# Second mixer of a three-layer fp32 kernel: q's norm moves into the softmax's exponential, the projections run q0, k, q1, v, the output weights' splits stand behind q's rotation, and the sine products read PSUM

## The chip, the cores and the metric

One core of one Trainium2 chip runs one program. The metric is the time of one execution in device microseconds; lower is better. Measurements of this kernel are told apart here from about 0.2% on (2.0 us).

## The reference, cut to what matters

The program is a chain of three layers on 256 tokens of 1024 channels, all in fp32. The change lies in the second layer's mixer, a grouped-query attention with 16 query heads and 4 key/value heads of 64 channels:

```python
def odd_mixer(x, mix_norm, w_qkv, q_norm, k_norm, w_out):
    Bsz, S, _ = x.shape
    proj = rms_norm(x, mix_norm) @ w_qkv
    q, k, v = jnp.split(proj, [GQA_Q_WIDTH, GQA_Q_WIDTH + GQA_KV_WIDTH], axis=-1)
    q = rms_norm(q.reshape(Bsz, S, GQA_HEADS, GQA_HEAD_DIM), q_norm)
    k = rms_norm(k.reshape(Bsz, S, GQA_KV_HEADS, GQA_HEAD_DIM), k_norm)
    v = v.reshape(Bsz, S, GQA_KV_HEADS, GQA_HEAD_DIM)
    cos, sin = axial_rope_tables(S)
    q = apply_rope(q, cos, sin)
    k = apply_rope(k, cos, sin)
    return gqa_block_attention(q, k, v) @ w_out
```

`rms_norm` divides each head by the root of its mean square (one factor per token and head) and multiplies by a gain; `apply_rope` turns neighbouring channels by an angle: a cosine product of each channel plus a sine product of its neighbour. The attention is softmax(q kT / 8) v over all 256 keys. After the mixer comes the layer's feed-forward block.

## The kernel before, in words

The tokens are two tiles of 128 (t = 0, 1). Every fp32 product with weights is made of three PE matmuls in fp32r (`mm3`, L121 to L123): weights and activations are each split into a rounded half (`wh`, `xTh`) and the rest (`wl`, `xTl`). `wload` (L103) loads four 128-row blocks of weights per DMA on SP's queue (`raw`, 3 buffers), then splits them in pairs: a cast on ACT (L112) and a subtraction on DVE (L113), into 6 buffers. `gemm` (L153) walks the 8 blocks of the 1024 input channels; at the end of each it calls `tick`, which runs work put off by `defer`, and at its end `done(t, acc)`.

The second mixer (L797 to L923) projects in three passes of 512 columns: k and v together (`okv`), then heads 0 to 7 of q (`oq`, c = 0), then heads 8 to 15 (c = 1). Each pass's `done` copies the sum out of PSUM with the token's norm as a factor (L840, L866), and `rope` (L813) squares it on ACT, sums the squares on DVE (L820), takes the power -1/2 on POOL (`gp_rms`, L188), makes the cosine products on POOL (L826) and the two halves of the sine products on DVE (L828), both from that copy in SBUF. The put-off `mid` adds the two (L870) and multiplies by the norm (L871; for k L848, twice). The put-off `fin` transposes on PE (`tq` L877, `tk` L854) and splits the result into `qS` (ACT cast L881, DVE subtraction L882) or `kh`, `kl`.

A unit of attention (`ga_unit` L888, `attn_unit` L309) handles two heads of one token tile: scores on PE (`sc_ga` L895, 2 PSUM buffers), negated maximum on DVE (`mx_ga` L328), exponential on ACT with the maximum as bias and a row sum (`p_ga` L335), reciprocal on DVE (L337), four transposes on PE (`pt_ga` L343), a copy on ACT (`pT_ga` L345), the value matmuls on PE (`o_ga` L354) and the scaled output on DVE (`ot` L356). `tq`, `tk`, `pt_ga` and `o_ga` share 2 PSUM buffers. `pipeline` runs 16 units, the three phases of a unit 0, 1 and 2 slots apart. After every four units `split_T` transposes their output (`tp_ot`, `mo`). The output projection (`oo`, weights `w_out_o`) fills in between units from the 13th slot on and ends the stage. The first two units start when 6 of the 8 blocks of the last projection are done.

The framework's scheduler fixes each engine's order when the kernel is built; every engine then works its queue off in order and waits at its head.

## Time and profile before

| | |
|---|---|
| median of 3 runs (lowest to highest) | 1008.73 us (1006.83 to 1009.10) |
| the profiled execution, its own time | 1009.89 us |
| span of that execution | 1008.1 us |
| PE busy | 978.6 us, 97% of the span |
| DVE, ACT, POOL busy | 65%, 56%, 10% |
| mean granted TensorE clock | 0.988 of full speed |
| second mixer, first projection matmul to the next layer's first | 399.95 to 503.70 us |

A span is the time from the first to the last instruction; the execution's own time is 1.8 us longer. A share of busy time is an average over stages with different limits, so what the change touches is read in the mixer's own stretch. The granted clock is 1.0 at the full 2.4 GHz and 0.5 at 1.2 GHz; a PE that is busy at half clock moves at half speed.

### The profile page before, as it was taken

What the parts mean: (1) busy time and instruction counts of PE and PEld (TensorE: products, weight loads), DVE (VectorE), ACT (ScalarE), POOL (GpSimd) and SP (SyncE); (2) the same over time, 40 slices, a digit from 0 to 9 for tenths busy, and PEclk for the clock granted to TensorE, in tenths of its full rate; (3) what the DMA queues carried; (4) which work ended last, traced back from release to release, by engine and by line L of the source; (5) the groups of instructions that cost most, each with busy time, mean ns of one, the idle gap of its engine ahead of it and who ended that gap; (6) DMA issues with size and microseconds to landing.
All of it is one profiled execution on the core that took longest, in us unless ns stands there. A gap on an engine that the chain in (4) does not pass through costs nothing.

```text
span 1008.1 us, 13120 instructions
## 1 busy us (share of the span) xinstructions
PE 978.6 (97%) x4926; PEld 816.5 (81%) x4926; DVE 650.9 (65%) x1038; ACT 560.6 (56%) x973; POOL 97.5 (10%) x161
## 2 busy tenths in 40 slices
PE   5999999999999999979999999999999999999998
PEld 4888888788888888869888888888888888888876
DVE  5668789776666555776676666555555976665455
ACT  6565778664445444567565444344675854454442
POOL 3130223110000001440010000001000300000000
PEclk9899999999999999989999999999999999999999
DMA  8546321545555455421345545546633565554541
GB/s 325 181 127 243 130 86 42 208 167 185 190 177 199 151 184 209 167 84 43 126 167 172 203 172 197 183 132 244 223 107 105 187 231 188 179 196 153 188 161 42
DMA packets 30535, 167.68 MB, mean 166 GB/s; under 512 B 3048, under 2 KB 8424, under 8 KB 12552
## 3 DMA queue, kind: packets, MB, share of 16 engines
q1 hardware_dynamic: 30472, 166.84, 47.8%
q8 instruction: 39, 0.64, 0.3%
q14 instruction: 24, 0.20, 0.1%
HBM read 165.71 MB, written 1.11 MB: 165 GB/s over the span
## 4 chain that ended last, share of the span: by engine, by line
PE 85%; DVE 7%; POOL 3%; issue 2%; ACT 2%; DMA 1%; SPq 0%; DVEq 0%; POOLq 0%; ACTq 0%
PE acc_fau L123 4%; PE acc_fbu L123 4%; PE acc_fau L122 4%; PE acc_fcu L122 4%; PE acc_fbu L122 4%; PE acc_fcu L121 4%; PE acc_fbu L121 4%; PE acc_fau L121 4%; PE acc_fcu L123 4%; PE acc_mpd L122 2%; PE acc_odd L123 2%; PE acc_mpd L123 2%; PE acc_mpd L121 2%; PE acc_odd L121 2%; PE acc_odd L122 2%; PE acc_fd L122 2%
## 5 line engine op out<-in xcount | busy, mean ns | idle before, releaser
L113 DVE TENSOR_TENSOR wl_fau<-raw_fau,wh_fau 128x1024 fp32r<-128x1024 f32 x44 | 53.8, 1223 | 39.8 <-ACT wh_fau L112 39.8
L113 DVE TENSOR_TENSOR wl_fbu<-raw_fbu,wh_fbu 128x1024 fp32r<-128x1024 f32 x44 | 53.8, 1223 | 39.0 <-ACT wh_fbu L112 39.0
L113 DVE TENSOR_TENSOR wl_fcu<-raw_fcu,wh_fcu 128x1024 fp32r<-128x1024 f32 x44 | 53.6, 1221 | 30.2 <-ACT wh_fcu L112 30.1
L123 PE MATMUL acc_fau<-wh_fau,xTl_f 128*128 128x512 f32 x176 | 70.6, 401 | 0.0
L123 PE MATMUL acc_fbu<-wh_fbu,xTl_f 128*128 128x512 f32 x176 | 70.5, 401 | 0.0
L123 PE MATMUL acc_fcu<-wh_fcu,xTl_f 128*128 128x512 f32 x176 | 70.0, 399 | 0.0
L112 ACT CAST wh_fau<-raw_fau 128x1024 fp32r<-128x1024 f32 x44 | 46.2, 1049 | 41.3 <-PE acc_fau L123 33.1
L122 PE MATMUL acc_fau<-wl_fau,xTh_f 128*128 128x512 f32 x176 | 68.9, 391 | 0.0
L122 PE MATMUL acc_fbu<-wl_fbu,xTh_f 128*128 128x512 f32 x176 | 68.8, 391 | 0.0
L121 PE MATMUL acc_fcu<-wh_fcu,xTh_f 128*128 128x512 f32 x176 | 68.8, 391 | 0.0
L122 PE MATMUL acc_fcu<-wl_fcu,xTh_f 128*128 128x512 f32 x176 | 68.7, 392 | 0.0
L121 PE MATMUL acc_fbu<-wh_fbu,xTh_f 128*128 128x512 f32 x176 | 68.7, 390 | 0.0
L121 PE MATMUL acc_fau<-wh_fau,xTh_f 128*128 128x512 f32 x176 | 68.7, 390 | 0.0
L112 ACT CAST wh_fbu<-raw_fbu 128x1024 fp32r<-128x1024 f32 x44 | 46.2, 1050 | 39.4 <-PE acc_fbu L123 32.9
L112 ACT CAST wh_fcu<-raw_fcu 128x1024 fp32r<-128x1024 f32 x44 | 46.3, 1053 | 30.3 <-PE acc_fcu L123 30.1
L113 DVE TENSOR_TENSOR wl_fd<-raw_fd,wh_fd 128x1024 fp32r<-128x1024 f32 x22 | 26.9, 1224 | 27.4 <-ACT wh_fd L112 27.4
L113 DVE TENSOR_TENSOR wl_mpd<-raw_mpd,wh_mpd 128x1024 fp32r<-128x1024 f32 x22 | 26.9, 1224 | 26.4 <-ACT wh_mpd L112 26.4
L113 DVE TENSOR_TENSOR wl_odd<-raw_odd,wh_odd 128x1024 fp32r<-128x1024 f32 x22 | 26.9, 1224 | 26.4 <-ACT wh_odd L112 26.4
L112 ACT CAST wh_fd<-raw_fd 128x1024 fp32r<-128x1024 f32 x22 | 23.1, 1049 | 29.4 <-PE acc_fd L123 24.1
L466 PE MATMUL xbc<-h,wh_xbc 128*128 128x256 f32 x128 | 38.9, 304 | 0.5 <-DVE xp L476 0.3
L112 ACT CAST wh_mpd<-raw_mpd 128x1024 fp32r<-128x1024 f32 x22 | 23.1, 1048 | 29.2 <-PE acc_mpd L123 23.9
L112 ACT CAST wh_odd<-raw_odd 128x1024 fp32r<-128x1024 f32 x22 | 23.1, 1049 | 29.2 <-PE acc_odd L123 23.9
(506 smaller groups left out, 2830.9 us busy)
## 6 DMA issues: line engine op xcount, KB each, us to landing
raw_fau<-in_w_dram SPq DMA_DIRECT2D x22, 1024.0 KB, 5.0
raw_fbu<-in_w_dram SPq DMA_DIRECT2D x22, 1024.0 KB, 5.2
raw_fcu<-in_w_gu_dram SPq DMA_DIRECT2D x22, 1024.0 KB, 5.0
raw_odd<-in_w_dram SPq DMA_DIRECT2D x10, 1024.0 KB, 4.9
raw_mpd<-in_w_dram SPq DMA_DIRECT2D x10, 1024.0 KB, 4.8
raw_fd<-in_w_dn_dram SPq DMA_DIRECT2D x10, 1024.0 KB, 4.9
raw_xbc<-in_w_xbc_dram SPq DMA_DIRECT2D x8, 1024.0 KB, 5.2
raw_eo<-in_w_out_e_dram SPq DMA_DIRECT2D x6, 1024.0 KB, 5.2
```

Source lines behind the costliest of these rows:

```text
L112: act.copy(wh[:, 0:n, 0:cols], raw[:, i:i + n, 0:cols])
L113: vec.tensor_tensor(out=wl[:, 0:n, 0:cols], in0=raw[:, i:i + n, 0:cols], in1=wh[:, 0:n, 0:cols].bitcast(F32), op=ALU.subtract)
L121: pe.matmul(acc, lhsT=x2[0], rhs=w2[0], start=start, stop=False)
L122: pe.matmul(acc, lhsT=x2[0], rhs=w2[1], start=False, stop=False)
L123: pe.matmul(acc, lhsT=x2[1], rhs=w2[0], start=False, stop=stop)
L466: pe.matmul(d, lhsT=wh[:, cs], rhs=h0[:, k, :], start=k == 0, stop=False)
```

## The change

It does six things, all in the second mixer:

- q is no longer multiplied by its norm. The norm (`rq8`) becomes the scale of the exponential (`scl`, `fac`), and the maximum is multiplied by it on POOL (`nb`, one small operation per unit).
- The sine products read the projection's sum in PSUM, not its copy; the tokens' norm is multiplied into the sine tables instead (four operations on POOL). They are written ahead of the square and its sum.
- The projections run in the order q heads 0 to 7 (512 columns), k (256 columns), q heads 8 to 15, v (256 columns); the first two units start after 6 of v's 8 blocks. `vv` becomes a tile of its own. k's second copy is made by ACT.
- The DVE subtractions of the output weights' first four pairs in each half (`ogen(0)`) are queued behind DVE's last subtraction of `qS`, c = 1 (`issue_after`, `last[1]`); their ACT casts are not.
- The put-off steps of q and k come at other ticks.
- The phases of a unit lie 0, 2 and 3 slots apart.

```diff
-    def wload(src, k0, kn, nm, cols=512):
+    def wload(src, k0, kn, nm, cols=512, behind=None):
...
-            vec.tensor_tensor(out=wl[:, 0:n, 0:cols], in0=raw[:, i:i + n, 0:cols],
-                              in1=wh[:, 0:n, 0:cols].bitcast(F32), op=ALU.subtract)
+            with tc.issue_after(behind) if behind is not None else nullcontext():
+                vec.tensor_tensor(out=wl[:, 0:n, 0:cols], in0=raw[:, i:i + n, 0:cols],
+                                  in1=wh[:, 0:n, 0:cols].bitcast(F32), op=ALU.subtract)
...
+            fac = [sign, sign]
+            if scl is not None:
+                nb = sm.tile([P, 2], F32, tag="nb", name=f"nb_{nm}", bufs=4)
+                gp.tensor_tensor(out=nb, in0=mx, in1=scl(), op=ALU.mult)
+                mx, fac = nb, [scl()[:, h:h + 1] for h in range(2)]
             for h in range(2):
-                act.activation(pvw[:, h, :], src[:, h, :], AF.Exp, bias=mx[:, h:h + 1], scale=sign,
+                act.activation(pvw[:, h, :], src[:, h, :], AF.Exp, bias=mx[:, h:h + 1], scale=fac[h],
                                accum_out=su[:, h:h + 1])
...
+                gp.tensor_scalar(out=S[:, t, :], in0=S[:, t, :], scalar1=rr[t], scalar2=None, op0=ALU.mult)
+
+        def rope(acc, src, nh, t, tab, nm):
...
+            for e in range(2):
+                vec.tensor_tensor(out=tv[:, :, e::2], in0=acc[:, :, 1 - e::2],
+                                  in1=S[:, t, e::2].unsqueeze(1).to_broadcast([P, nh, 32]), op=ALU.mult)
+            gp.tensor_tensor(out=qv, in0=src, in1=C[:, t, :].unsqueeze(1).to_broadcast([P, nh, 64]), op=ALU.mult)
...
-                for e in range(2):
-                    vec.tensor_tensor(out=kd[:, :, e, :], in0=qv, in1=r8, op=ALU.mult)
+                vec.tensor_tensor(out=kd[:, :, 0, :], in0=qv, in1=r8.unsqueeze(2).to_broadcast([P, 4, 64]), op=ALU.mult)
+                act.copy(kd[:, :, 1, :], kd[:, :, 0, :])
                 defer(3, fin)
...
-            defer(4, mid)
+            defer(2 + t, mid)
...
                 def mid():
                     vec.tensor_tensor(out=qv, in0=qv, in1=tv, op=ALU.add)
-                    vec.tensor_tensor(out=qv, in0=qv, in1=r8, op=ALU.mult)
-                    defer(2, fin)
+                    defer(1, fin)
...
-                        vec.tensor_tensor(out=qS[c][e][lo, t], in0=tv[hi], in1=qS[c][e][hi, t].bitcast(F32),
-                                          op=ALU.subtract)
-                defer(3 + 2 * t, mid)
+                        last[c] = vec.tensor_tensor(out=qS[c][e][lo, t], in0=tv[hi],
+                                                    in1=qS[c][e][hi, t].bitcast(F32), op=ALU.subtract).ins
+                defer(2 + 2 * t, mid)
...
-        run(gemm(a["w_qkv_o"][0], KD, xf, done_kv, "okv"))
-        run(gemm(a["w_qkv_o"][1], KD, xf, done_q(0), "oq0"))
-        og = gemm(a["w_qkv_o"][2], KD, xf, done_q(1), "oq1")
+                yield from gemm(a["w_out_o"][n], KD, xT_acc(mo), done, f"oo{n}", kfirst=k0, klast=k0 + 4, accs=accs[n],
+                                behind=lambda: last[1] if k0 == 0 else None)
+
+        run(gemm(a["w_q_o"][0], KD, xf, done_q(0), "oq0"))
+        run(gemm(a["w_k_o"][0], KD, xf, done_k, "ok", cols=256))
+        run(gemm(a["w_q_o"][1], KD, xf, done_q(1), "oq1"))
+        og = gemm(a["w_v_o"][0], KD, xf, done_v, "ov", cols=256)
         run(og, 6)
         ga = pipeline([ga_unit(c, t, pr) for c in range(2) for t in range(NT) for pr in range(4 * c, 4 * c + 4)],
-                      (0, 1, 2))
+                      (0, 2, 3))
```

How the change moves instructions, in each engine's fixed order. Outside the second mixer the orders are the same. The lines of the changed kernel lie 2 to 22 further down.

**DVE, q's rotation and what follows it.** Before, heads 0 to 7: the two products with the norm, then three subtractions of output weights (`wl_oo`) ahead of and between those of `qS`, and only then the first maxima.

```order
L871 TENSOR_TENSOR rq_q_0_3970<-rq_q_0_3970,r_q_0_3967 128x512
L871 TENSOR_TENSOR rq_q_1_3985<-rq_q_1_3985,r_q_1_3982 128x512
L113 TENSOR_TENSOR wl_oo_2_4461<-raw_oo_0_4454,wh_oo_2_4460 128x1024
L113 TENSOR_TENSOR wl_oo_0_4586<-raw_oo_0_4583,wh_oo_0_4585 128x1024
L882 TENSOR_TENSOR qS_3752<-tq_0_4030,qS_3752 64x512
L113 TENSOR_TENSOR wl_oo_2_4590<-raw_oo_0_4583,wh_oo_2_4589 128x1024
L882 TENSOR_TENSOR qS_3753<-tq_0_4030,qS_3753 64x512
L328 TENSOR_REDUCE mx_ga_0_4076<-sc_ga_0_4070 128x2
L882 TENSOR_TENSOR qS_3752<-tq_1_4061,qS_3752 64x512
L328 TENSOR_REDUCE mx_ga_1_4088<-sc_ga_1_4082 128x2
L337 RECIPROCAL su_ga_0_4077<-su_ga_0_4077 128x2
```

Changed, heads 8 to 15, with what each row waits for: the sine products (`rt_q`) read `acc_oq` and wait for ACT, whose copy reads the same PSUM tile; the sums (`rq_q`) wait for POOL's cosine products; no product with the norm follows.

```order
L836 TENSOR_TENSOR rt_q_0_4089<-acc_oq_0_3996,Sgq 128x256 [waits Activation_49]
L836 TENSOR_TENSOR rt_q_0_4089<-acc_oq_0_3996,Sgq 128x256
L836 TENSOR_TENSOR rt_q_1_4104<-acc_oq_1_3997,Sgq 128x256 [waits Activation_49]
L843 TENSOR_REDUCE s_q_0_4095<-rj_q_0_4093 128x8 [waits Activation_49]
L836 TENSOR_TENSOR rt_q_1_4104<-acc_oq_1_3997,Sgq 128x256
L890 TENSOR_TENSOR rq_q_0_4088<-rq_q_0_4088,rt_q_0_4089 128x512 [waits DVE_49,Pool_49]
L843 TENSOR_REDUCE s_q_1_4110<-rj_q_1_4108 128x8 [waits Activation_49]
L890 TENSOR_TENSOR rq_q_1_4103<-rq_q_1_4103,rt_q_1_4104 128x512 [waits DVE_49,Pool_49]
```

The rows right behind these, also of the changed kernel: first maxima, q's four subtractions, and from there the output weights' subtractions between the maxima.

```order
L331 TENSOR_REDUCE mx_ga_0_4200<-sc_ga_0_4194 128x2 [waits PE_49]
L901 TENSOR_TENSOR qS_3760<-tq_0_4141,qS_3760 64x512 [waits Activation_49]
L901 TENSOR_TENSOR qS_3760<-tq_1_4163,qS_3760 64x512 [waits Activation_49]
L331 TENSOR_REDUCE mx_ga_1_4214<-sc_ga_1_4208 128x2 [waits PE_49]
L901 TENSOR_TENSOR qS_3761<-tq_0_4141,qS_3761 64x512 [waits Activation_49]
L901 TENSOR_TENSOR qS_3761<-tq_1_4163,qS_3761 64x512 [waits Activation_49]
L345 RECIPROCAL su_ga_0_4201<-su_ga_0_4201 128x2 [waits Activation_49]
L115 TENSOR_TENSOR wl_oo_0_4544<-raw_oo_0_4541,wh_oo_0_4543 128x1024 [waits DMAHW1_49]
L345 RECIPROCAL su_ga_1_4215<-su_ga_1_4215 128x2 [waits Activation_49]
L331 TENSOR_REDUCE mx_ga_2_4242<-sc_ga_2_4236 128x2 [waits PE_49]
L331 TENSOR_REDUCE mx_ga_3_4263<-sc_ga_3_4257 128x2 [waits PE_49]
```

What moved: before, splits of the output weights stood ahead of the first units' q; now they stand in the middle of the first units, six of them between the third and the tenth unit's rows.

**PE, the opening of the attention.** Before, the transposes of q's second tile are followed at once by the first scores, with matmuls of the last projection between the units.

```order
L877 MATMUL tq_1_4061<-cst,rq_q_1_3985 128x128 x4
L895 MATMUL sc_ga_0_4070<-kh,qS_3752 128x256
L895 MATMUL sc_ga_0_4070<-kl,qS_3752 128x256
L895 MATMUL sc_ga_0_4070<-kh,qS_3752 128x256
L895 MATMUL sc_ga_0_4070<-kl,qS_3752 128x256
L121 MATMUL acc_oq_0_3990<-wh_oq_6_4045,xTh_od 128x512
L122 MATMUL acc_oq_0_3990<-wl_oq_6_4046,xTh_od 128x512
L895 MATMUL sc_ga_1_4082<-kh,qS_3753 128x256
```

Changed, the end of v's projection and what follows: the weights' transposes (`pt_ga`) and the third unit's scores, with no projection matmul left to stand between them until the output projection's first rows, some fifty rows further on.

```order
L123 MATMUL acc_ov_4117<-wh_ov_4178,xTh_od 128x256
L124 MATMUL acc_ov_4117<-wl_ov_4179,xTh_od 128x256
L125 MATMUL acc_ov_4117<-wh_ov_4178,xTl_od 128x256
L351 MATMUL pt_ga_0_4250<-cst,p_ga_0_4199 128x128
L914 MATMUL sc_ga_2_4236<-kh,qS_3758 128x256
L914 MATMUL sc_ga_2_4236<-kl,qS_3758 128x256
L914 MATMUL sc_ga_2_4236<-kh,qS_3758 128x256
L914 MATMUL sc_ga_2_4236<-kl,qS_3758 128x256
L351 MATMUL pt_ga_0_4250<-cst,p_ga_0_4199 128x128 x3
L351 MATMUL pt_ga_1_4271<-cst,p_ga_1_4213 128x128 x2
```

ACT in the same place of the changed kernel: between the transposes of heads 8 to 15 and the end of the first unit's second exponential stand four casts of q and one of the output weights.

```order
L900 CAST qS_3760<-tq_0_4141 64x512 [waits PE_49]
L900 CAST qS_3760<-tq_1_4163 64x512 [waits PE_49]
L113 CAST wh_oo_4_4738<-raw_oo_4_4736 128x1024 [waits DMAHW3_49]
L343 ACTIVATE p_ga_0_4199,su_ga_0_4201<-sc_ga_0_4194,nb_ga_0_4203,r_q_0_3855 128x256 [waits Pool_49]
L900 CAST qS_3761<-tq_0_4141 64x512 [waits DVE_49]
L900 CAST qS_3761<-tq_1_4163 64x512 [waits DVE_49]
L343 ACTIVATE p_ga_0_4199,su_ga_0_4201<-sc_ga_0_4194,nb_ga_0_4203,r_q_0_3855 128x256
```

What moved: the first units no longer wait for their own q (it was turned a projection earlier), but the projection matmuls that stood between units are spent before them.

## Rows read from the trace of the kernel before

**Rows 1.** The table of busy time by stretch: first the whole second mixer, from its first projection matmul to the first matmul of the next feed-forward layer. Columns: the stretch (us from the span's start), its length, then busy time and number of instructions of PE, of PE's weight loads, of DVE, ACT and POOL, the granted TensorE clock as a share of full speed, the busy share of the DMA engines, GB/s.

```profile
399.95:503.70 103.75, 98.52 (x554) 84.77 (x553) 73.10 (x133) 65.86 (x149) 25.37 (x35) 0.93 0.31 106
```

**Rows 2.** The same table for four stretches inside it.

```profile
428.80:438.10 9.30, 5.43 (x29) 3.87 (x27) 7.36 (x10) 4.12 (x6) 3.05 (x3) 0.97 0.31 102
438.10:444.20 6.10, 6.10 (x18) 4.97 (x19) 4.07 (x7) 4.12 (x12) 0.20 (x1) 0.50 0.53 191
444.20:451.20 7.00, 5.63 (x44) 5.06 (x43) 6.26 (x14) 5.77 (x15) 5.43 (x6) 0.99 0.00 0
451.20:457.50 6.30, 6.30 (x32) 6.26 (x31) 4.16 (x10) 2.89 (x10) 1.10 (x1) 0.50 0.00 0
```

**Rows 3.** The list of what PE waited for between 398 and 506 us (engine, line, what it waited for: us in total, times, longest), whole.

```profile
PE sc_ga L895 <- DVE qS L882: 2.4, 2, 1.6
PE tq L877 <- DVE rq_q L871: 1.5, 1, 1.5
PE o_ga L354 <- DVE ot L356: 0.9, 1, 0.9
PE pt_ga L343 <- DVE ot L356: 0.5, 1, 0.5
```

**Rows 4.** The chain of waits that ended last, between 428 and 460 us. Columns: start, us, engine, tile, line, number of instructions.

```profile
432.97 2.35 DVE wl_oo L113 x2
...
435.36 0.68 DVE qS L882
...
436.07 1.22 DVE wl_oo L113
...
437.33 0.70 DVE qS L882
```

**Rows 5.** The instructions of q's rotation, from the answers on its tiles: sine products on DVE, cosine products on POOL, their sum, the sum of squares, the power that turns it into the norm. Columns: line, engine, operation, out<-in, count, shortest/median/longest in ns, first and last start, forms.

```profile
L828 DVE TENSOR_TENSOR rt_q<-q,Sgq x8: 407/411/1517, 424.6 to 448.0; 128x256 f32<-128x256 f32 x8
...
L826 POOL TENSOR_TENSOR rq_q<-q,Cgq x4: 1277/1288/1488, 423.9 to 445.3; 128x512 f32<-128x512 f32 x4
...
L870 DVE TENSOR_TENSOR rq_q<-rq_q,rt_q x4: 671/680/685, 428.1 to 454.1; 128x512 f32<-128x512 f32 x4
...
L820 DVE TENSOR_REDUCE s_q<-rj_q x4: 666/670/672, 426.8 to 449.2; 128x8 f32<-128x512 f32 x4
...
L188 POOL TENSOR_TENSOR r_q<-ms_q,mhalf x4: 1636/1688/1984, 428.0 to 450.3; 128x8 f32<-128x8 f32 x4
```

**Rows 6.** The timelines of DVE (first three rows) and POOL (last row) around 423 to 430 us. Columns: start, us from the first start to the last end, engine, line, operation, out<-in, shape, count.

```profile
423.45 1.28 DVE L858 TENSOR_TENSOR kl<-tk,kh 128x512 fp32r<-128x512 f32 x2
424.65 2.23 DVE L828 TENSOR_TENSOR rt_q<-q,Sgq 128x256 f32<-128x256 f32 x2
...
428.07 1.29 DVE L870 TENSOR_TENSOR rq_q<-rq_q,rt_q 128x512 f32<-128x512 f32 x2
...
423.86 2.74 POOL L826 TENSOR_TENSOR rq_q<-q,Cgq 128x512 f32<-128x512 f32 x2 [4.53 <-ACT q L866]
```

**Rows 7.** PE's timeline, the same columns: two matmuls of a 512-column projection, 28 starts apart, two neighbours of a 256-column projection in the first mixer, and one turn of an attention unit (four transposes, eight value matmuls, the next scores).

```profile
404.98 0.39 PE L121 MATMUL acc_okv<-wh_okv,xTh_od 128*128 128x512 f32 x1
...
411.33 0.39 PE L122 MATMUL acc_okv<-wl_okv,xTh_od 128*128 128x512 f32 x1
...
33.10 0.28 PE L467 MATMUL xbc<-l,wh_xbc 128*128 128x256 f32 x1
33.22 0.28 PE L468 MATMUL xbc<-h,wl_xbc 128*128 128x256 f32 x1
...
462.51 0.60 PE L343 MATMUL pt_ga<-cst,p_ga 128*128 128x128 f32 x4
462.94 1.00 PE L354 MATMUL o_ga<-kv,pT_ga 128*128 128x64 f32 x8
463.76 0.36 PE L895 MATMUL sc_ga<-kh,qS 128*128 128x256 f32 x1
```

**Rows 8.** The forms of one attention unit outside PE (exponential, maximum, scaled output, copy of the transposed weights), of the split of a pair of output-weight blocks (ACT, DVE) and of q's split after its transposes (ACT, DVE); columns as in rows 5.

```profile
L335 ACT ACTIVATE p_ga<-sc_ga,mx_ga x32: 459/474/481, 438.8 to 483.5; 128x256 f32<-128x256 f32 x32
...
L328 DVE TENSOR_REDUCE mx_ga<-sc_ga x16: 669/691/692, 438.1 to 481.9; 128x2 f32<-128x512 f32 x16
...
L356 DVE TENSOR_TENSOR ot<-o_ga,su_ga x16: 261/291/292, 448.5 to 487.4; 128x128 f32<-128x128 f32 x16
...
L345 ACT COPY pT_ga<-pt_ga x16: 583/585/589, 441.9 to 485.0; 128x512 f32<-128x512 f32 x16
...
L112 ACT CAST wh_oo<-raw_oo x8: 1029/1044/1052, 420.1 to 484.0; 128x1024 fp32r<-128x1024 f32 x8
...
L113 DVE TENSOR_TENSOR wl_oo<-raw_oo,wh_oo x8: 1202/1217/1224, 422.3 to 485.8; 128x1024 fp32r<-128x1024 f32 x8
...
L881 ACT CAST qS<-tq x8: 579/580/582, 431.4 to 466.2; 64x512 fp32r<-64x512 f32 x8
...
L882 DVE TENSOR_TENSOR qS<-tq,qS x8: 683/688/694, 435.4 to 467.4; 64x512 fp32r<-64x512 f32 x8
```

**Rows 9.** ACT's copy of q out of PSUM (timeline, columns as in rows 6), the landing time of the output weights' loads (the answer on their tile), and the smallest two-input operation on POOL (columns as in rows 5).

```profile
423.10 0.69 ACT L866 ACTIVATE q<-acc_oq,r_od 128x512 f32<-128x512 f32 x1 [0.94 <-PE acc_oq L123]
...
DMA to landing us min/median/max: 5.0/5.0/5.2
...
L263 POOL TENSOR_TENSOR sst_od<-ss_od x2: 187/573/959, 404.2 to 405.3; 128x1 f32<-128x1 f32 x2
```

More of the change, by code (lines that the diff above doesn't have):

```diff
@@ L1 @@
 import math
-from contextlib import ExitStack
+from contextlib import ExitStack, nullcontext
 import concourse.bass as bass
@@ L151, in run, with gemm @@
                 n -= 1
-    def gemm(src, K, xf, done, nm, touter=0, kfirst=0, klast=None, accs=None, cols=512, pre=None):
+    def gemm(src, K, xf, done, nm, touter=0, kfirst=0, klast=None, accs=None, cols=512, pre=None, behind=None):
         klast = K if klast is None else klast
@@ L160, in gemm @@
             kn = min(4, klast - k0)
-            ws = pre[k0:k0 + kn] if pre is not None else wload(src, k0, kn, nm, cols)
+            ws = pre[k0:k0 + kn] if pre is not None else wload(src, k0, kn, nm, cols, behind and behind())
             for i in range(kn):
@@ L307, in ffn_up, with attn_unit @@
         return lambda k, t: (hT[k // 2][0][:, t, k % 2, :], hT[k // 2][1][:, t, k % 2, :])
-    def attn_unit(pool, nm, qk, nk, bias, vf, oap, after=None):
+    def attn_unit(pool, nm, qk, nk, bias, vf, oap, after=None, scl=None):
         KT = nk // P
@@ new lines, in rope, with done_v, done_k @@
+            gp_rms(s8, nh, 64, nm, r8)
+            return q, qv, tv, r8
+        kS = [O.tile([P, 4, T], F32R, tag=f"k{s}", name=f"k{s}") for s in "hl"]
+        vv = [O.tile([P, 256], F32, tag=f"vv{t}", name=f"vv{t}") for t in range(NT)]
+        def done_v(t, acc):
+            act.activation(vv[t], acc[:, 0:256], AF.Copy, scale=rr[t])
+        def done_k(t, acc):
+            ks = O.tile([P, 512], F32, tag="q2", name=f"k{t}", bufs=4)[:, 0:256]
+            act.activation(ks, acc[:, 0:256], AF.Copy, scale=rr[t])
```

45 lines of the change are left out of this document (21 added, 24 removed).

## The prediction

> **What bounds the kernel now.** PE is busy 97% of the span, and outside the second mixer no engine's order changes, so the question is what PE's time in that mixer consists of. I read the table of busy time by stretch first [rows 1]: 103.75 us, PE busy 98.52, so 5.23 idle, at a mean clock of 0.93. The same table cut finer [rows 2] shows where the clock was low: 438.10 to 444.20 and 451.20 to 457.50, both at 0.50 with PE busy throughout (6.10 of 6.10, 6.30 of 6.30). A busy PE at half clock takes twice the time, so these cost 3.05 and 3.15, together 6.2. Without idle time and slow clock the same matmuls would take 103.75 − 5.23 − 6.2 = **92.3 us**. Both slow stretches follow a stretch in which PE had holes: 5.43 busy of 9.30 before the first, 5.63 of 7.00 before the second.
>
> The list of PE's waits [rows 3] names the holes: 2.4 for `qS`, 1.5 for q's second tile (`tq` behind L871), 0.9 and 0.5 for scaled outputs, 5.3 in all. The chain of waits [rows 4] says why `qS` was late: three output-weight subtractions (2.35 for two, then 1.22; 3.57 us of DVE) stood ahead of and between q's own subtractions of 0.68 and 0.70.
>
> **The change, part by part.**
>
> *Projections in 256 columns.* k and v need 96 matmuls of 256 columns instead of 48 of 512. From start to start these take 0.12 and (411.33 − 404.98) / 28 = 0.227 us [rows 7]: 11.5 against 10.9, so +0.6, all on PE. The floor becomes 92.9.
>
> *Order of the output weights' subtractions.* The 3.57 us no longer stand ahead of the first units' q, and heads 0 to 7 are turned a whole projection before they are used. The 2.4 of waits for `qS` goes. The six subtractions, 1.22 each [rows 8], now stand among the maxima of the third to tenth unit; see (d) and (e).
>
> *Norm in the exponential.* Four DVE products go, of the form of L870: 0.68 each [rows 5], two per projection. The power on POOL (1.69) leaves the path from the sum of squares to the transposes; only the first exponential needs it. The wait of 1.5 for L871 goes. POOL gets one `nb` per unit, between 0.19 and 0.57 each by its smallest two-input operation [rows 9]; it stands between a unit's maximum and its exponential, with two or three slots to spare, and costs nothing except in the opening (d). The four scalings of the sine tables run on an idle POOL before the first rotation, with a projection of 48 matmuls (10.9) over them: nothing.
>
> *Sine products from PSUM.* A pair's half took 0.41 at the shortest and 1.52 at the longest [rows 5]. The slow pair, 2.23 for two, ran while POOL's cosine products ran (423.86 to 426.60); two `kl` subtractions, one of whose inputs is in PSUM, ran beside the same POOL rows in 1.28, or 0.64 each, as the PSUM-fed `qS` form does at 0.69 [rows 6, 8]. So I expect 0.41 for each. But the sine products wait for ACT's copy of the same PSUM tile (the order shows the wait), so they start no earlier than before. The Trainium skill ("SBUF — State Buffer", "Who interferes with whom") says that a DVE instruction with two SBUF inputs contends with a GpSimd instruction that reads SBUF, and one with at most one such input does not. The trace agrees as far as it goes (1.52 against 0.64). The rule also speaks against a full gain, since the sums L870 keep two SBUF inputs: by it the time is the forecast's, and by the pair of sums at 1.29 in (a) it is that of the second rival.
>
> *New and remaining waits of PE.* I walk each place; E is the end of the projection that feeds the rotation.
> (a) Turn of heads 0 to 7 under k's projection. ACT's copy ends at about E + 0.3 for the first tile (it starts before the second tile's matmuls end; 0.69 each, [rows 9]), POOL's two cosine products of 1.29 end at E + 1.6 and E + 2.9. The first sum has two SBUF inputs, and I assume it is held up by POOL's second product as the sine product was: ready at E + 3.6. PE reaches `tq` after 25 matmuls, 3.0. Wait 0.6, and 0.1 for the second tile: **0.7**. Against it stands that two sums, begun at 428.07, took 1.29 beside POOL's power, begun at 428.0 [rows 5, 6]; then (a) is 0.
> (b) k's transposes: no wait is listed before; now the same chain stands under a 512-column pass, with ACT's second copy added. Between 0 and the 1.6 that is the longest wait in the list; I take **0.6**, the value of (a).
> (c) Heads 8 to 15 under v. The output weights' load lands late (5.0 us, [rows 9]) and its ACT cast (1.04, [rows 8]) stands ahead of q's copies on ACT, so the chain of (a) is 1.04 later: E + 4.64, against 32 matmuls, 3.84. **0.8**.
> (d) Opening of the attention. From the end of `tq`'s second tile PE has 18 matmuls of 256 columns, 2.16, until it needs the first unit's scores consumed (six of the first two units, then v's last two blocks, 12). In the same time ACT has four casts of q (0.58 each), one of the weights (1.04) and the first unit's two exponentials (0.47 each) [rows 8], in the order that the changed kernel's ACT rows show: 4.3. Wait **2.1**. DVE's part of the chain, a maximum of 0.69, then `nb`, lies beside the first casts. Bounds: 0.9, the longest wait for a unit's own steps now [rows 3], and 3.2, with one more weight cast in the way or its load late by as much.
> (e) The units over the six subtractions. From the first maximum to the sixth subtraction DVE has 10 maxima (6.9), 4 `qS` (2.8), 7 outputs (2.0), 6 subtractions (7.3) and one copy of the form of an output's split (0.7): 19.7. PE has there, at full clock, about 16.1: 10 units at the 1.61 that [rows 7] show from the start of the transposes to the end of the scores (462.51 to 464.12). The difference is 3.6, of which (d) holds 2.1; the other **1.5** falls behind it, first at late `ot`, then at `tp_ot`.
> Sum of waits: 0.7 + 0.6 + 0.8 + 2.1 + 1.5 = **5.7**, about what it is now (5.23). Bounds: 2.5, if (a) and (b) are 0, (c) 0.1, (d) 0.9 and (e) 1.5; 8.5, if (b) is 1.6, (d) 3.2 and (e) 2.2 (the difference of 3.6 with a unit's maximum more, less the usual 2.1).
>
> *The clock.* In the trace it fell after holes. The holes of the two turns are short now (a to c); those of the opening are not. I take one slow stretch of the present length, 6.2, behind (d). It costs 3.1, but at half clock DVE catches up on PE, so 1.2 of the waits in (e) go: **1.9** net.
>
> Stage: 92.9 + 5.7 + 1.9 = **100.5**, 3.25 less than 103.75. The profiled execution, 1009.89, would become 1006.6; it lies 1.16 above the median of the runs shown, and the difference carries over to that: 1008.73 − 3.25 = **1005.5 us**.
>
> **The rivals.**
> *No slow stretch.* The holes are shorter and spread out, and the clock stays up: 92.9 + 4.0 (waits midway between 2.5 and 5.7) = 96.9, −6.85, **1001.9**. For it: the hole of 2.4 and 1.5 that preceded the first fall is gone. Against: (d) is as large.
> *The sums are not held up.* (a) is 0 and (c) 0.1, so 1.4 less than the forecast: **1004.1**. For it: the pair at 1.29. Against: the sine products at 1.52, with the same two kinds of inputs.
> *No change.* Two slow stretches of 6.2 each again; they cost 6.2 and swallow some 2 of the waits: 92.9 + 5.7 + 4.2 = 102.8, and with (b) at 1.6, 103.8: **1008.8**. For it: before, the second fall came in the middle of the first units, behind waits of 0.9 and 0.5 for `ot`, and (e) makes such waits larger.
> *Slower: half clock through the opening.* Between v's end and the output projection PE has only short matmuls, 64 to 256 columns, and each unit may end in a wait behind a 1.22 subtraction. If the clock stays low for three times the present stretch, 18.6 us, that costs 9.3; at half clock PE no longer waits at (e), and (a) to (d) leave 4.2: 92.9 + 4.2 + 9.3 = 106.4, +2.65, **1011.4**. It decides where the slow time costs more than 103.75 + 2.0 − 92.9 − 4.2 = 8.65, from 17.3 us of it on. For it: [rows 2] have PE busy for 6.30 of 6.30 at 0.50 amid those very units. Against: from 457.5 on the same units ran at full clock.
>
> **How the numbers follow.** Chances: forecast 0.42, no slow stretch 0.22, sums free 0.06, no change 0.17, slower 0.13. A measurement tells some 0.2%, 2.0 us, from no change. Of the forecast's 0.42 I count 0.32 as faster and 0.10 as same (waits near 8). Faster: 0.32 + 0.22 + 0.06 = 0.60; same: 0.10 + 0.17 = 0.27; slower 0.13. The range runs from the lowest waits without a slow stretch, 92.9 + 2.5 = 95.4, −8.35, 1000.4, to the highest waits with two slow stretches that swallow (e)'s 2.2 of them, 92.9 + 8.5 + 6.2 − 2.2 = 105.4, +1.65, 1010.4. It leaves out most of the slower rival and a corner of the first.
>
> **What would show it.** The list of PE's waits no longer has `sc_ga` behind `qS`, nor `tq` above 0.9; the sine products stand at 0.41 each beside POOL's cosine products; the sums show 0.68 if free, over 1 if held up; the first `pt_ga` waits some 2 us; the six subtractions lie between maxima, with waits for `ot` or `mx_ga` behind them; one stretch at 0.5 of some 6 us, instead of two. The prediction is wrong if the slow stretches are two or more, if the opening's waits exceed 5 us together, or if the loss appears in the output projection, which I take as unchanged.

## The result and the profile after

The changed kernel takes **1000.59 us** (median of 4 runs, 1000.40 to 1002.18) against 1008.91 (4 runs): ratio **0.9925, 95% interval 0.9908 to 0.9942**, 8.3 us less. The forecast was 1005.5 in a range of 1000.4 to 1010.4: the direction holds, the time lies at the range's lower edge, and the size is that of the first rival (1001.9). Profile against profile the span fell from 1008.1 to 1000.4, by 7.7 us. Of these 5.2 lie in the second mixer and about 2.6 in a place that the prediction did not look at. Ahead of the second mixer both profiles have the same half clock (6.8 us from 25 us on, 3.4 us from 93 us on), so it is not in the difference.

The table of busy time by stretch, changed kernel: the whole mixer (to be read against [rows 1]), then the last eight microseconds before the first units run freely, and what follows. Columns as in [rows 1].

```profile
399.35:497.87 98.52, 93.74 (x601) 82.06 (x600) 67.72 (x130) 70.07 (x157) 29.93 (x55) 1.00 0.35 123
...
434.60:437.90 3.30, 2.56 (x23) 2.41 (x22) 2.25 (x4) 3.13 (x6) 2.96 (x5) 1.00 0.23 97
437.90:442.40 4.50, 2.48 (x20) 2.08 (x19) 4.11 (x8) 4.00 (x11) 1.58 (x3) 1.00 0.00 0
442.40:457.00 14.60, 13.21 (x103) 11.56 (x101) 12.72 (x26) 12.64 (x37) 2.23 (x7) 1.00 0.43 145
```

103.75 became 98.52. The clock is 1.00 in every stretch: both half-clock stretches of [rows 2], which cost 6.2, are gone. PE idles 4.78 instead of 5.23, and its busy time at full clock rose from 92.3 to 93.7. So −6.2 (clock), −0.45 (waits), +1.45 (busy) make −5.2.

What PE waited for in the mixer, whole list (to be read against [rows 3]):

```profile
PE pt_ga L351 <- DVE qS L901: 1.9, 1, 1.9
PE tq L896 <- DVE rq_q L890: 1.2, 2, 0.7
PE sc_ga L914 <- ACT p_ga L343: 0.6, 1, 0.6
PE o_ga L362 <- DVE mol L231: 0.5, 1, 0.5
PE o_ga L362 <- ACT pT_ga L353: 0.2, 1, 0.2
PE tk L871 <- ACT kd L865: 0.2, 1, 0.2
```

The waits for `qS` ahead of scores are gone. The longest hole is now the one in front of the first transposes. The chain of waits around it (start, us, engine, tile, line, number of instructions):

```profile
432.22 2.57 POOL rq_q L838 x2
...
435.48 1.64 POOL r_q L190
...
437.49 1.64 POOL r_q L190
439.13 0.17 POOL nb_ga L340
...
439.32 0.66 ACT p_ga L343 x2
...
440.00 1.07 ACT qS L900 x2
441.09 1.75 ACT p_ga L343 x6
```

The first exponential waits for `nb`, which on POOL stands behind the power of a norm that this unit does not need; then two casts of q stand between its two exponentials. `pt_ga` takes the PSUM buffer of `tq`, which is free when the subtraction behind those casts has read it; that is why the list names `qS`.

The rotation's forms (columns as in [rows 5], against which they are to be read): sine products, sums, then the exponential, which had 474 ns.

```profile
L836 DVE TENSOR_TENSOR rt_q<-acc_oq,Sgq x8: 414/416/426, 411.6 to 433.9; 128x256 f32<-128x256 f32 x8
...
L890 DVE TENSOR_TENSOR rq_q<-rq_q,rt_q x4: 676/900/1166, 413.6 to 435.9; 128x512 f32<-128x512 f32 x4
...
L343 ACT ACTIVATE p_ga<-sc_ga,nb_ga,r_q x32: 554/565/619, 439.3 to 475.4; 128x256 f32<-128x256 f32 x32
```

The other 2.6 us: each of the three down projections behind a feed-forward block (`odd`, `mpd`, `fd`) got 0.8 to 1.0 us shorter, though no engine's order changed there. First and last rows of `mpd` (line, count, shortest/median/longest ns, first and last start): the kernel before, then the changed one.

```profile
L121 PE MATMUL acc_mpd<-wh_mpd,hh_fb x88: 390/393/477, 629.5 to 691.5; 128*128 128x512 f32 x88
...
L123 PE MATMUL acc_mpd<-wh_mpd,hl_fb x88: 390/393/483, 629.9 to 692.0; 128*128 128x512 f32 x88
```

```profile
L123 PE MATMUL acc_mpd<-wh_mpd,hh_fb x88: 392/394/481, 623.8 to 685.0; 128*128 128x512 f32 x88
...
L125 PE MATMUL acc_mpd<-wh_mpd,hl_fb x88: 388/392/481, 624.3 to 685.4; 128*128 128x512 f32 x88
```

From the first to the last start that is 62.5 (629.5 to 692.0) against 61.6 (623.8 to 685.4), for the same 264 matmuls at a clock of 1.00.

Executions of one and the same kernel differ in how often the clock falls: 79 runs of the kernel before, taken beside the experiments, lie at 1003.2 to 1003.6 us (5 runs, mean granted clock 0.996), 1004.3 to 1007.1 (29 runs, 0.993) and 1007.5 to 1009.7 (45 runs, 0.988 to 0.991), with a median of 1007.8, by which the gain is 7.2 us, and e9's ten runs lie at 996.8 to 998.3 and at 1004.1 to 1004.9.

So an experiment is read by its profile first: the mixer's length, how long the clock's records put it at half clock, the sum of PE's waits in it, one down projection. The ratio goes by the runs of the kernel before that were taken beside the experiment. For the kernel before the records say 13.7 us; the stretches in [rows 2] are cut a little shorter, to 12.4.

| kernel | median us | ratio to before [95%] | mixer | at half clock | waits | `mpd` |
|---|---|---|---|---|---|---|
| before | 1008.91 | | 103.7 | 13.7 | 5.3 | 62.5 |
| changed | 1000.59 | 0.9925 [0.9908, 0.9942] | 98.5 | 0 | 4.6 | 61.6 |
| e1 splits free | 1003.69 | 0.9958 [0.9945, 0.9972] | 100.9 | 6.8 | 4.7 | 61.6 |
| e2 norm on q | 1007.86 | 1.0010 [0.9995, 1.0024] | 101.9 | 0 | 7.8 | 62.7 |
| e3 before, splits behind | 1006.45 | 0.9986 [0.9977, 0.9994] | 101.2 | 6.8 | 5.9 | 62.5 |
| e4 longer hole | 1006.83 | 0.9984 [0.9976, 0.9993] | 104.1 | 6.8 | 7.9 | 61.6 |
| e5 before, tiles moved | 1002.97 | 0.9973 [0.9955, 0.9991] | 99.9 | 3.4 | 5.7 | 61.6 |
| e6 changed, tiles moved | 1004.37 | 0.9978 [0.9966, 0.9991] | 99.6 | 3.4 | 4.2 | 62.5 |
| e7 old sequence | 1012.33 | 1.0051 [1.0033, 1.0070] | 109.4 | 17.1 | 8.3 | 61.6 |
| e8 casts behind | 999.98 | 0.9927 [0.9910, 0.9944] | 97.8 | 0 | 3.5 | 61.6 |
| e9 e8, tiles moved | 1001.16 | 0.9941 [0.9918, 0.9964] | 97.7 | 0 | 3.5 | 61.1 |
| e10 distances 0, 1, 2 | 1001.14 | 0.9944 [0.9929, 0.9960] | 97.9 | 0 | 4.1 | 61.6 |
| e11 before, norm and splits | 1002.57 | 0.9955 [0.9940, 0.9970] | 100.8 | 10.2 | 3.9 | 61.6 |
| e12 sines from SBUF | 1009.16 | 1.0032 [1.0018, 1.0046] | 106.8 | 10.2 | 7.9 | 61.6 |

### The profile page after: what moved, and what is told of

Read it like the earlier page. It is cut to its first block, busy times and chain, and to the rows that moved or that the text cites. A ratio compares the mean times of both kernels' runs of the same rounds, so it can differ in the third digit from the quotient of the medians.

```text
span 1000.4 us, 13270 instructions
## 1 busy us (share of the span) xinstructions
PE 971.5 (97%) x4974; PEld 813.2 (81%) x4974; DVE 645.7 (65%) x1036; ACT 564.6 (56%) x981; POOL 102.2 (10%) x181
## 4 chain that ended last, share of the span: by engine, by line
PE 85%; DVE 6%; POOL 3%; ACT 2%; issue 2%; DMA 0%; DVEq 0%; POOLq 0%; ACTq 0%
PE acc_fbu L125 4%; PE acc_fau L125 4%; PE acc_fau L124 4%; PE acc_fbu L124 4%; PE acc_fcu L124 4%; PE acc_fcu L125 4%; PE acc_fau L123 4%; PE acc_fbu L123 4%; PE acc_fcu L123 4%; PE acc_mpd L123 2%; PE acc_odd L125 2%; PE acc_mpd L125 2%; PE acc_odd L123 2%; PE acc_odd L124 2%; PE acc_mpd L124 2%
```

## The experiments

The theory to be tested: the mixer gains because PE's holes ahead of the first units became short enough for the clock to stay up (the long ones bring it down); each part of the change matters as far as it shortens one of them. The rival in general: one part (the sequence, or the norm) does it, and the rest is idle. One thing speaks against the theory from the start: the longest hole of the kernel before is 1.6 [rows 3], shorter than the 1.9 that the changed kernel keeps at full clock. The experiments below show what a longer hole does (e1, e3, e4, e12); why the kernel before loses the clock at its shorter ones they do not show.

**e1, the splits free.** The rule on the output weights' subtractions is taken out (it holds four pairs in all, two in each half, not four in each half).

```diff
-                                behind=lambda: last[1] if k0 == 0 else None)
+                                behind=None)
```

> The changed kernel without the rule that keeps the output weights' subtractions behind q's last one. Two of them (1.22 us each) then stand ahead of q's second rotation and of its four subtractions. Theory (the stage gains because PE's holes ahead of the first units are short enough that the clock stays up, and the place of these subtractions is what shortens them): the hole ahead of the first pt_ga grows from 1.9 to about 3.3 us, a stretch at half clock comes back, 1003 to 1005 us. Rival A (the order of the projections and the norm do it, the subtractions' place matters little): the hole grows, but what is moved forward is saved among the units, no slow stretch, 1000.2 to 1001.5 us.

Measured: 1003.69, 3.1 more than the changed kernel. Two stretches of the mixer, columns as in [rows 1], and the list's first row:

```profile
436.00:442.00 6.00, 2.87 (x21) 2.19 (x19) 5.70 (x10) 5.90 (x14) 2.31 (x5) 1.00 0.48 175
442.00:449.00 7.00, 6.84 (x32) 6.51 (x32) 4.76 (x9) 4.08 (x15) 1.43 (x3) 0.52 0.46 152
```

```profile
PE pt_ga L351 <- ACT p_ga L343: 3.2, 2, 2.7
```

The hole grows to 2.7, and 6.8 us at half clock follow. The waits' sum is that of the changed kernel (4.7 against 4.6); the mixer's 2.3 more come with the clock. It is not this profile alone: all twelve runs had a mean clock of 0.991 or less, the changed kernel's four 0.994 or more. Theory.

**e2, the norm on q.** DVE multiplies the sum by the norm again; the exponential has no scale.

```diff
                     vec.tensor_tensor(out=qv, in0=qv, in1=tv, op=ALU.add)
+                    vec.tensor_tensor(out=qv, in0=qv, in1=rq8[c, t].unsqueeze(2).to_broadcast([P, 8, 64]), op=ALU.mult)
                     defer(1, fin)
...
-                             scl=lambda: rq8[c, t][:, 4 * (i % 2) + e:4 * (i % 2) + e + 3:2])
```

> The changed kernel with q multiplied by its norm on DVE again, ahead of the transposes, and no norm in the exponential. Theory: POOL's power (1.65 each, two per projection, behind cosine products of 1.3) is back between the sums and the transposes; the second rotation's tq is late by 2 to 3 us instead of 0.7, in the stretch that already holds the hole of 1.9, and the clock falls: 1004 to 1007 us. Rival A (the order of the projections alone hides the norm, since q heads 0 to 7 are turned a projection early): 1000.5 to 1002 us, no slow stretch.

Measured: 1007.86. The first rows of the list of PE's waits:

```profile
PE tq L897 <- DVE rq_q L891: 4.9, 3, 1.8
PE sc_ga L915 <- ACT p_ga L343: 1.2, 4, 0.5
```

The time lies 0.9 above the theory's range, and the mechanism is another: the waits grew by 3.2 (4.6 to 7.8) and the mixer by 3.4, at full clock throughout. Many holes, none above 1.8, did not bring the clock down, though their sum is among the four largest in the table. Some 3.3 us more are the three down projections (`mpd` 62.7 against 61.6), since this kernel's tiles lie elsewhere (e5).

**e3, the kernel before with its splits held behind DVE's last subtraction of heads 0 to 7** (with the `behind` of `wload` and `gemm` as in the change).

```diff
...
+                                behind=lambda: last[0] if k0 == 0 else None)
```

> The kernel before with one part of the change: the first output weights' subtractions stand behind DVE's last subtraction of q heads 0 to 7. Theory: the 2.4 us of waits for qS go, and with them the first slow stretch (3.05 us); the wait of 1.5 for tq stays, waits for ot may grow by 1 and keep the second slow stretch: 1003.5 to 1005.5 us. Rival A (the gain needs the projections' order and the norm): the wait moves to ot or to the chain over the norm, both slow stretches stay, 1007 to 1009 us.

Measured: 1006.45, ratio 0.9986, an interval that leaves no change out by little.

```profile
PE pt_ga L344 <- ACT p_ga L336: 4.2, 1, 4.2
PE tq L880 <- DVE rq_q L874: 0.8, 1, 0.8
```

The waits for `qS` went from 2.4 to 0.2, and a hole of 4.2 in front of the first transposes took their place; one slow stretch comes with it (442.4 to 449.2 at 0.50), the second did not come. Between theory and rival: the wait moves, as the rival says, but one slow stretch less is 2.5 us.

**e4, a longer hole.** Two more powers on POOL ahead of the first `nb`.

```diff
             gp_rms(s8, nh, 64, nm, r8)
+            if nm == "q1_1":
+                for z in range(2):
+                    gp.tensor_tensor(out=zz, in0=r8, in1=mhalf[:, 0:nh], op=ALU.pow)
...
+        zz = O.tile([P, 8], F32, tag="zz", name="zz")
```

> The changed kernel with two more powers on POOL (results unused, about 1.65 us each) between the second rotation's norm and the first unit's product with it, so that the first exponential is late by some 3.3 us more and the hole ahead of the first pt_ga is some 5 us instead of 1.9. Nothing else is changed. Theory (the length of PE's hole decides whether the clock falls): a stretch at half clock follows, 3.3 of hole and 3.1 of slow clock more, 1006 to 1008 us. Rival B (the clock doesn't depend on this hole, but on what ran before it): the hole alone, 1003 to 1004.5 us.

Measured: 1006.83, 6.2 more than the changed kernel.

```profile
442.40:448.20 5.80, 1.78 (x15) 1.57 (x14) 2.58 (x4) 1.98 (x5) 5.03 (x5) 1.00 0.00 0
448.20:455.00 6.80, 5.49 (x25) 5.23 (x26) 4.04 (x7) 5.52 (x15) 0.39 (x2) 0.51 0.01 2
```

The hole is 5.3 instead of 1.9, and a half-clock stretch of 6.8 comes with it. Besides the two powers and the small tile `zz` that they write nothing was changed, and all 13 runs had a mean clock of 0.993 or less, the changed kernel's four 0.994 or more; so the hole brought it. Theory. The profiled execution took 1012.32; it also has 13.7 us at half clock in the first mixer, far ahead of the edit (last section).

**e5 and e6, tiles moved in SBUF.** As the programs are laid out, the only operands of the down projections' matmuls that moved are the stationary ones, `hh` and `hl`: from offset 127008 in a partition to 127328, modulo 256 bytes from 32 to 96. e5 moves them so in the kernel before, by an unused tile; e6 adds 192 bytes to the changed kernel (offset 32 modulo 256 again).

```diff
+    pad = sm.tile([P, 80], F32, tag="pad", name="pad", bufs=1)
+    gp.memset(pad, 0.0)
```

> The kernel before with one unused tile of 320 bytes per partition in the pool of small tiles, so that the feed-forward blocks' hidden tiles (hh, hl) and all tiles behind them in SBUF lie 320 bytes further on, exactly where the changed kernel has them. No engine's order changes. Theory P (the 0.9 us that each of the three down projections lost between the two kernels, 62.5 against 61.6, comes from where these tiles lie): down projections 61.6 each, mixer unchanged at 103.7 with its two slow stretches, 1005.5 to 1006.5 us. Rival C (it comes from something else in the change, such as the program's length): down projections 62.5, 1008 to 1009 us.

> The changed kernel with an unused tile of 192 bytes in the same pool, which puts hh and hl at the same offset modulo 256 bytes as in the kernel before (32 instead of 96). Theory P: down projections 62.5 each again, mixer unchanged at 98.6, 1002.8 to 1003.8 us. Rival C: 1000.2 to 1001.2 us.

`mpd` in e5, then in e6:

```profile
L121 PE MATMUL acc_mpd<-wh_mpd,hh_fb x88: 388/392/481, 629.9 to 691.0; 128*128 128x512 f32 x88
...
L123 PE MATMUL acc_mpd<-wh_mpd,hl_fb x88: 388/394/481, 630.3 to 691.5; 128*128 128x512 f32 x88
```

```profile
L123 PE MATMUL acc_mpd<-wh_mpd,hh_fb x88: 390/393/479, 624.4 to 686.4; 128*128 128x512 f32 x88
...
L125 PE MATMUL acc_mpd<-wh_mpd,hl_fb x88: 390/393/479, 624.9 to 686.9; 128*128 128x512 f32 x88
```

61.6 in the old kernel with the new places, 62.5 in the new kernel with the old ones: theory P, with the down projections in both cases as forecast. Which of the moved tiles does it was not tried; that it is `hh` and `hl` follows from their being the only moved operands.

The times lie beside their forecasts, e5's below, e6's 0.6 above. e5's forecast started from 1008.9, but the kernel before took 1006.34 in the runs beside e5: 3.4 more than e5, of which 2.6 are the down projections. e5's profiled execution took 1008.36. Its mixer came out at 99.9, with only 3.4 us at half clock, although its order and its waits (5.7) are nearly those of before; but it spent 13.7 us at half clock in the first mixer. e6, with the changed kernel's order and hole (1.9), had 3.4 us at half clock in the second mixer as well, and 99.6. So at holes of this size the clock falls in some executions and not in others.

With the tiles' places exchanged, the old and the new order differ by 0.3 in the mixer, where the profiles of the kernel before and of the changed one differ by 5.2. How much of those 5.2 belongs to the new order, and how much to where the clock happened to fall, one profile of each does not say. By the table's ratios the places alone bring 2.7 us (e5, interval 0.9 to 4.5) and the new order alone 2.2 (e6, 0.9 to 3.4), together some 5; the 8.3 were measured against runs of the kernel before at 1008.9, the later ones have medians of 1006.3 to 1008.3.

**e7, the old sequence.** k, v, q heads 0 to 7, q heads 8 to 15; the rest as changed.

```diff
+        run(gemm(a["w_k_o"][0], KD, xf, done_k, "ok", cols=256))
+        run(gemm(a["w_v_o"][0], KD, xf, done_v, "ov", cols=256))
         run(gemm(a["w_q_o"][0], KD, xf, done_q(0), "oq0"))
-        run(gemm(a["w_k_o"][0], KD, xf, done_k, "ok", cols=256))
-        run(gemm(a["w_q_o"][1], KD, xf, done_q(1), "oq1"))
-        og = gemm(a["w_v_o"][0], KD, xf, done_v, "ov", cols=256)
+        og = gemm(a["w_q_o"][1], KD, xf, done_q(1), "oq1")
```

> The changed kernel with the projections in the old sequence (k, v, q heads 0 to 7, q heads 8 to 15; k and v still 256 columns each), the first units after 6 of the last projection's 8 blocks. Theory (turning q heads 0 to 7 a projection early is what keeps the opening's hole short): PE waits 2 to 3 us at the first scores or transposes, the clock falls once, 1003 to 1006 us. Rival D (with the norm in the exponential and the splits behind, q's turn is short enough to be hidden in any order, and 512-column matmuls lie between the units): no slow stretch, 999 to 1001.5 us.

Measured: 1012.33, slower than the kernel before, and beyond the theory's range.

```profile
PE sc_ga L914 <- ACT p_ga L343: 3.4, 3, 1.5
PE tk L871 <- ACT kd L865: 2.5, 2, 2.0
```

The turn of k no longer has a long pass over it: v's 256-column matmuls are spent before `kd` is ready, and half clock follows (413.6 to 417.0); then 13.7 us at half clock from 447.7 on, after the waits for exponentials. The sequence is needed, and in two places, of which the theory named one.

**e8, ACT's casts behind too.** The casts of the first output weights wait for ACT's last cast of q.

```diff
+    last_act = [None]
...
-            act.copy(wh[:, 0:n, 0:cols], raw[:, i:i + n, 0:cols])
+            with tc.issue_after(last_act[0]) if behind is not None else nullcontext():
+                act.copy(wh[:, 0:n, 0:cols], raw[:, i:i + n, 0:cols])
...
-                        act.copy(qS[c][e][hi, t], tv[hi])
+                        last_act[0] = act.copy(qS[c][e][hi, t], tv[hi]).ins
```

> The changed kernel with the ACT casts of the output weights' first four pairs held behind ACT's last cast of q, as the DVE subtractions are held behind DVE's. Theory (the hole of 1.9 ahead of the first pt_ga is ACT's queue, one weight cast of 1.04 ahead of the first exponential): the hole shrinks to 0.8 to 1.2 us, 999.3 to 1000.2 us, unless the output projection has to wait for its later weights. Rival E (POOL's second power, which ends 0.2 us before the first exponential, sets it): the hole stays above 1.5, 1000.3 to 1001.2 us.

Measured: 999.98; mixer 97.8.

```profile
PE pt_ga L354 <- ACT p_ga L346: 1.7, 2, 0.9
PE sc_ga L917 <- ACT p_ga L346: 0.6, 1, 0.6
PE pt_ga L354 <- DVE su_ga L348: 0.5, 1, 0.5
```

In place of the hole of 1.9 stand two: 0.8 ahead of the first transposes, then 0.9; the waits fell from 4.6 to 3.5. ACT's timeline at the first of the two, and POOL's and DVE's at the second (columns as in [rows 6]):

```profile
433.48 2.52 ACT L903 CAST qS<-tq 64x512 fp32r<-64x512 f32 x4 [2.15 <-PE tq L899]
436.02 1.05 ACT L116 CAST wh_oo<-raw_oo 128x1024 fp32r<-128x1024 f32 x1
437.10 0.56 ACT L346 ACTIVATE p_ga<-sc_ga,nb_ga,r_q 128x256 f32<-128x256 f32 x1
...
438.24 1.23 POOL L343 TENSOR_TENSOR nb_ga<-mx_ga,r_q 128x2 f32<-128x2 f32 x1 [1.86 <-DVE mx_ga L334]
...
438.19 1.22 DVE L118 TENSOR_TENSOR wl_oo<-raw_oo,wh_oo 128x1024 fp32r<-128x1024 f32 x1
```

The time is as the theory has it, its reason only in part: one weight cast still stands ahead of the first exponential (436.02). What went are the casts ahead of q's (four of them in the changed kernel, 430.51 to 436.83), so that all four casts of q are done before the first exponential. The second hole waits for the second unit's exponential, whose `nb` took 1.23 beside a weight subtraction. Against both kernels: faster than the one before (0.9927), not to be told from the changed one by its time.

**e9, e8 with 64 bytes more** (offset 160 modulo 256).

```diff
+    pad = sm.tile([P, 16], F32, tag="pad", name="pad", bufs=1)
+    gp.memset(pad, 0.0)
```

> The kernel of e8 (the changed kernel with the weights' casts held behind q's) with an unused tile of 64 bytes, so that hh and hl lie at offset 160 modulo 256 bytes (32 and 224 gave down projections of 62.5, 96 gave 61.6). Theory P1 (there are two kinds of places, and those well inside are good): down projections 61.6, 999 to 1000.5 us as e8. Rival P2 (each place has its own cost): down projections above 62 or below 61.3, 1001.5 to 1002.5 or under 999 us.

`mpd` is shorter still, 61.1 (619.6 to 680.7):

```profile
L126 PE MATMUL acc_mpd<-wh_mpd,hh_fb x88: 388/389/478, 619.6 to 680.2; 128*128 128x512 f32 x88
...
L128 PE MATMUL acc_mpd<-wh_mpd,hl_fb x88: 388/389/482, 620.1 to 680.7; 128*128 128x512 f32 x88
```

Rival P2: 32 and 224 give 62.5 and 62.7, 96 gives 61.6, 160 gives 61.1. Its median, 1001.16, lies between the two groups of its runs (mean clock 0.995 and 0.988) and says little; where the second group lost its time is in no profile of e9.

**e10, the distances.** Phases 0, 1 and 2 slots apart.

```diff
-                      (0, 2, 3))
+                      (0, 1, 2))
```

> The changed kernel with the phases of a unit 0, 1 and 2 slots apart, as before. Theory (the longer distance covers the longer chain from scores to transposes, maximum 0.69, nb 0.2, two exponentials of 0.56 and 0.19 each, some 2.4 against one turn of 1.6): PE waits for exponentials at every unit, 0.3 to 0.8 each, 1003 to 1010 us, with or without slow clock. Rival F (the scheduler orders PE by readiness, so the program's distance hardly shows): 1000 to 1001.5 us.

Measured: 1001.14, mixer 97.9. Rival F: this part is worth nothing here.

**e11, the kernel before with the norm in the exponential and the splits behind.** Edits as in e3 and in the change.

> The kernel before with two parts of the change alone: the norm in the exponential, and the first weights' subtractions behind DVE's last subtraction of q heads 0 to 7. The projections' sequence, the sine products and the distances stay as before; hh and hl lie as in the changed kernel. Theory (q heads 0 to 7 must be turned a projection early for a short hole): a wait of 3 us or more at the first transposes or scores stays, one slow stretch, 1002.5 to 1005 us. Rival G (these two parts are the whole gain): no slow stretch, mixer at most 98.6, 999.5 to 1001 us.

Measured: 1002.57, 3.7 less than the kernel before in the runs beside it; 2.6 of that are the tiles' places. The mixer is 100.8, with the smallest waits but two (3.9; the longest 1.9) and yet 10.2 us at half clock (439.6 to 449.8). Theory as to the time, not as to the mechanism: no hole of 3 is there.

**e12, the sine products from ACT's copy.**

```diff
-                gp.tensor_scalar(out=S[:, t, :], in0=S[:, t, :], scalar1=rr[t], scalar2=None, op0=ALU.mult)
+                pass
...
-                vec.tensor_tensor(out=tv[:, :, e::2], in0=acc[:, :, 1 - e::2],
+                vec.tensor_tensor(out=tv[:, :, e::2], in0=src[:, :, 1 - e::2],
```

> The changed kernel with the sine products read from ACT's copy in SBUF again (the sine tables without the token's norm); all else as changed. Theory (beside POOL's cosine product a sine product from SBUF takes up to 1.5 instead of 0.42, so the sums come later): the two waits of tq grow by 0.5 to 1.2 us together, 1001 to 1002.5 us, and up to 3 more if the clock falls. Rival H (the sums are held up by POOL's second cosine product in any case, so the time of the sine products ahead of them is hidden): 1000.2 to 1001 us.

Measured: 1009.16, 8.6 more than the changed kernel and slower than the one before. DVE's timeline over the second rotation, changed kernel, then e12 (columns as in [rows 6]), and e12's first wait:

```profile
432.18 1.09 DVE L836 TENSOR_TENSOR rt_q<-acc_oq,Sgq 128x256 f32<-128x256 f32 x3 [2.94 <-ACT q L885]
...
433.88 0.42 DVE L836 TENSOR_TENSOR rt_q<-acc_oq,Sgq 128x256 f32<-128x256 f32 x1
434.21 1.12 DVE L890 TENSOR_TENSOR rq_q<-rq_q,rt_q 128x512 f32<-128x512 f32 x1
```

```profile
433.37 3.58 DVE L836 TENSOR_TENSOR rt_q<-q,Sgq 128x256 f32<-128x256 f32 x4 [3.19 <-ACT q L885]
...
437.48 1.27 DVE L890 TENSOR_TENSOR rq_q<-rq_q,rt_q 128x512 f32<-128x512 f32 x2
```

```profile
PE tq L896 <- DVE rq_q L890: 5.9, 2, 4.1
```

From SBUF the four halves take 3.58 beside POOL's cosine products (2.92 for two), from PSUM 1.51 (1.09 and 0.42). The transposes of heads 8 to 15 wait 4.1 instead of 0.7, the clock falls behind them and once more among the units. Both answers that were expected missed the size.

## Why the prediction was right or wrong

- **What bounds the kernel**: right. The ledger (busy at full clock, waits, half clock) is what the result moved along, and the half clock was its largest item.
- **256 columns**: 0.12 from start to start, as taken. But the busy time at full clock rose by 1.45, not 0.6. Where the other 0.8 is was not settled; each hole adds the modelled end of a matmul to "busy", and there are more, shorter pieces.
- **The splits' place**: the waits for `qS` went, as said. e1 prices it: 2.3 in the mixer, by the clock.
- **The norm**: the wait for L871 went; e2 prices it at 3.4 in the mixer, nearly all of it waits. Missed: an exponential with a scale per row takes 0.565 instead of 0.474, 32 times on ACT, and `nb` may take 1.04 instead of 0.20 (below). The Trainium skill ("ScalarE: Activation LUTs", "What ACT_TABLE_LOAD costs") puts about 93 ns on each operand given per partition; the trace agrees with 91.
- **The sine products**: 0.416 each beside POOL, as read from the rows. In the sum they stood at nothing, because they start no earlier. This was the worst-sized term: by e12 the part is worth 8.3 us of mixer, part of it by the clock (10.2 us at half clock), since the two tiles' halves lie one behind the other ahead of the first sum: all four count there (3.58 in e12).
- **(a) to (e)**: sums held up, as assumed: 1.17 and 1.12 for the first of each pair, while POOL's second cosine product runs, 0.68 for the second. The Trainium skill ("SBUF — State Buffer", "Who interferes with whom") describes it so, and this trace agrees on both halves: one SBUF input 0.416 without exception, two inputs up to 1.17. The waits: (a) 0.5 (taken 0.7), (b) 0.2 (0.6), (c) 0.7 (0.8), (d) 1.9 (2.1), (e) 1.3 (1.5); 4.6 against 5.7. In (d) the size came out for a partly different reason: not ACT's queue alone, but POOL's second power ahead of `nb` (two more powers there lengthen the hole by 3.4, e4) and the PSUM buffer of `tq` stand in the chain; with q's casts out of the way earlier the hole is 0.8, and another of 0.9 takes its place (e8).
- **The clock**: the step that failed. "One slow stretch of the present length" behind (d) did not come; the first rival had it, at 0.22. With it the mixer's balance closes: 100.5 forecast, +0.8 busy, −0.9 waits, −1.9 clock, 98.5 measured. Why the clock stayed up is open: the reason that the first rival gave, that the holes are shorter and spread out, does not hold for the longest one (1.9 against 1.6 before), and e6, with the same order and the same hole, had 3.4 us at half clock.
- **Outside the mixer**: "outside the second mixer no engine's order changes" was true and the conclusion drawn from it, that nothing changes there, was wrong: 2.6 us by where two kinds of tiles lie. Of the 4.9 us between the forecast and the measured time 2.0 lie in the mixer and 2.6 here. The range had no term for the latter; that 1000.59 still lies inside it, 0.2 from its edge, is luck.
- **The distances** were never priced; e10 says they were worth nothing.
- **The rivals**: half clock through the opening, 17.3 us of it as the point of decision, is nearly what e7 shows (17.1 us, 13.7 of it in the opening; 1012.33), in another version of this kernel.

The parts do not add up: undone one by one they cost 2.3 (e1), 3.4 (e2), 10.9 (e7), 8.3 (e12) and nothing (e10) of the mixer, together several times the 5.2 that all of them brought. Each late chain opens a hole of its own, and where the clock falls behind it (e1, e7, e12) its price comes whole. With the clock up, the old mixer would be about as long as the new one (103.7 − 6.2 = 97.5 against 98.5): by these profiles, what the change brings in the mixer is the clock.

## What to carry to other kernels

Make the ledger with the clock as an item of its own, with both of its outcomes priced, and remove first the longest wait of PE in one piece: those of 2.7 us and more brought half clock in each of the four profiles that have one, and the waits' sum said nothing of it. Holes of 1.5 to 2.0 are no safe side: take several profiles before a stretch at half clock, or its absence, is put down to an edit. An edit that moves no instruction elsewhere may still move tiles: compare the length of stages that the change does not touch before the whole difference is explained by the stage that it does. A term that is "hidden because it starts no earlier" should be priced once with everything that stands in line with it.
